# Splitting the selected and local branches' query and key banks over 128 rows in a fused attention and FFN layer

## The chip, the cores and the metric

The kernel runs on one core of a Trainium2 chip. The metric is the device time of one execution in microseconds (us), taken as the median of several runs. A core has TensorE (PE, with its weight loads PEld), VectorE (DVE), ScalarE (ACT), GpSimd (POOL) and SyncE (SP), each working through its own instructions in order, and 16 DMA engines that move data for the queues the engines issue to.

## The reference

One decoder layer on x of 512 rows by 1024 columns, in fp32. A normalised input goes through one wide projection; its columns feed four groups of four heads, which share one output projection; a gated FFN with a causal convolution of width 3 follows.

```python
h = _rms_norm(x, attn_pre_norm[l])
(mq, mk, mv, nq, nkc, nvc, nks, nvs, nkw, nvw, ngate,
 dq, dk, dv, sq, sk, sv) = jnp.split(h @ w_in[l], splits, axis=-1)
o_moba = _moba_attention(...)     # block-sparse, 4 heads of 64
o_nsa  = _nsa_attention(...)      # compressed + selected + window keys; one key head for 4 query heads
o_diff = _diff_attention(...)     # differential: softmax minus lambda times softmax, heads of 32
o_swa  = _swa_attention(...)      # local window of 128 with sinks; 2 key heads for 4 query heads
mix = concatenate([o_moba, o_nsa, o_diff, o_swa], -1)
x = x + _rms_norm(mix @ w_out[l], attn_post_norm[l])
h = _rms_norm(x, ffn_pre_norm[l])
x = x + _rms_norm(_conv_ffn(h, ...), ffn_post_norm[l])
```

Below, NSA is the selected branch, SWA the local one.

## The kernel before, in words

**Precision.** Every fp32 operand is kept as a pair: hi, the value rounded to the matmul's format, and lo, the remainder. A product is three matmuls (hi·hi, lo·hi, hi·lo; `mm3`, L405 to L407 when it is a projection). ACT writes hi, DVE (for some weights POOL) writes lo.

**Weights.** SP loads a unit of weights into a `raw` tile (L91; two buffers, so a load waits until both engines that split the one before last are done with it). ACT makes hi (L152), DVE and POOL lo (L157), into one of four `wu` slots. FFN weights come as `pair` tiles of 1 MB (L104); POOL adds blocks of them into a tile of tag "sum" (L177, two buffers), ACT and DVE split them (L191, L194).

**First half.** A generator yields the projection units group by group (fill_moba, fill_nsa, fill_diff, fill_swa, fill_out). Each unit is 24 matmuls into a PSUM bank; when it ends, small closures that empty the bank are queued (`later`) and are run off one at a time between the matmuls that follow. Attention tasks are woven in at fixed rates: scores (L1012 with the hi of the keys, L1013 with the lo; L1069 for differential heads), softmax (mask and maximum on DVE L955, exponential on ACT L956, normalisation on POOL L948), transposes (L980), weighted sums (L991), combination. NSA's compressed keys need 32 small fp32 products (L733, 31 columns wide). A scheduler then fixes each engine's order from its own simulation of the program, so that fewer or shorter steps on one engine move instructions on others too.

**How a bank of queries or keys is emptied.** A bank holds two heads of 64 rows. For queries, `q_stack` (L475) makes one tile per head that holds hi in one half of its 128 rows and lo in the other: two ACT operations of 64x512 (L481) and two DVE operations (L485) that also scale. For keys, `k_stack` (L490) makes hi in 64 rows (ACT, L498), copies them into the other 64 rows by a DMA on ACT's queue (L499), and puts lo in a second tile whose other half POOL sets to zero (L503, DVE L504). MoBA's four banks, NSA's key bank and two query banks, and SWA's two query banks and key bank are emptied in this way. The differential heads (`narrow_stack`, L823) already do it otherwise: one ACT operation over all 128 rows into a tile `parts` (L833), one DVE operation over 128 rows (L839), and SP DMAs that place the pieces of 32 rows (L830). Their `parts` tiles also have tag "sum", two buffers.

**Second half.** The rest of the output projection, two norms and the FFN, whose products L1319 to L1321 run on `pair` weights.

Of the kernel before, what the change touches and what calls it, by code (L numbers as in the profile page):

```python
# [29 lines left out]
def f32(ap):  # L30
    return ap.bitcast(F32)
# [199 lines left out]
def kernel(  # L231
# [258 lines left out]
    def k_stack(ps, dst, kls, put):  # L490
# [14 lines left out]
            put.append(ts_[a])  # L505
        return [lambda: hi(0), lambda: hi(1), lambda: lo(0), lambda: lo(1)]

    def v_steps(ps, v, v3, t, extra=None):

        dst = v[:, t, :].rearrange("p (r x d) -> p r x d", r=2, x=4)  # L510
        src = ps[:, 0:256].rearrange("p (r x d) -> p r x d", r=2, x=2)
        d3 = v3[:, t, :, :]
        s3 = ps[:, 256:384].rearrange("p (n d) -> p n d", n=2)

        def a0():
            act.activation(dst[:, :, 0::3, :], src, AF.Copy)
            act.activation(d3[:, :, 0:64], s3, AF.Copy)

        def a1():
            act.activation(d3[:, :, 128:192], s3, AF.Copy)  # L520
            if extra:
                extra()

        def b0():
            vec.tensor_sub(dst[:, :, 1:3, :], src, f32(dst[:, :, 0::3, :]))

        def b1():
            vec.tensor_sub(d3[:, :, 64:128], s3, f32(d3[:, :, 0:64]))
        return [a0, a1, b0, b1]
# [90 lines left out]
    pool.memset(pair, 0.0)  # L620
    pool.memset(pair[0:64, 0:1], 1.0)
    pool.memset(pair[64:128, 1:2], 1.0)
    dscale = tab.tile([128, 2], F32, name="dscale")
    for h in range(4):
        pool.memset(dscale[64 * (h % 2):64 * (h % 2) + 64, h // 2:h // 2 + 1], qscale(2, h, 32))
    nsink = tab.tile([128, 4], F32, name="nsink")
    keep(vec.tensor_scalar(nsink, sink, -1.0, None, ALU.mult))
    lprod = tab.tile([128, 2, 32], F32, name="lprod")
# [47 lines left out]
    def fill_nsa():  # L676
# [22 lines left out]
        ps = yield from fm_unit()  # L699
        kls = [tt("kl"), tt("kl")]  # L700
        nks = []
        later(*k_stack(ps, (0, 0), kls, nks))
        later(lambda: nk.extend(zip(nks, kls)))
        mm_done()

# [18 lines left out]
                    vec.tensor_copy(g[:, h, :], g[:, 0, :])  # L724
        for n in range(2):
            ps = yield from fm_unit()
            later(*q_stack(ps, (0, 0), [qscale(1, 2 * n + a, 64) for a in range(2)], nq))
            mm_done()
            while len(xxs) <= n:
                pop()  # L730
# [89 lines left out]
        vec.tensor_sub(ct[1], ps, f32(ct[0]))  # L820
        cmp_["v"], cmp_["p"] = vc, ct

    def narrow_stack(ps, scale, places, twice, put):  # L823


        ts_ = [tt("dd") for _ in range(4)]
        parts = [wst.tile([128, S], F32R, tag="sum", name=nm("parts"), bufs=2) for _ in range(2)]

        def place(n, c, row):
            sp.dma_start(f32(ts_[c][row:row + 32]), f32(parts[n][32 * c:32 * c + 32]))  # L830

        def hi():
            act.activation(parts[0], ps, AF.Copy, scale=scale)  # L833
            for c in range(4):
                place(0, c, 0)
                place(0, c, twice)

        def lo():
            vec.scalar_tensor_tensor(parts[1], ps, scale, f32(parts[0]), ALU.mult, ALU.subtract)  # L839
            for c in range(4):  # L840
                place(1, c, places)
                put.append(ts_[c])
        return [hi, lo]

    def fill_diff():
        for p in range(2):
            ps = yield from fm_unit()
            later(*narrow_stack(ps, dscale[:, p:p + 1], 32, 64, dq))
            mm_done()
            ps = yield from fm_unit()  # L850
            later(*narrow_stack(ps, 1.0, 64, 32, dk))
            mm_done()
# [6 lines left out]
    def fill_swa():  # L859
        for p in range(2):  # L860
            ps = yield from fm_unit()
            later(*q_stack(ps, (64 * p, 64 * p), [qscale(3, 2 * p + a, 64) for a in range(2)], sq_))
            mm_done()
        ps = yield from fm_unit()
        late["skl"] = [tt("kl"), tt("kl")]
        later(*k_stack(ps, (0, 64), late["skl"], sk))
        mm_done()
        yield "swa"

# [616 lines left out]
```

## Time and profile before

| what | value |
|---|---|
| median of 3 runs | 813.96 us (813.44 to 815.26) |
| the profiled execution, its own time | 814.86 us |
| its span, first to last instruction | 813.0 us |
| PE / PEld busy | 776.9 us (96%) / 710.5 us (87%) |
| DVE busy | 658.4 us (81%) |
| ACT busy | 439.2 us (54%) |
| POOL busy | 339.2 us (42%) |
| mean granted TensorE clock | 0.987 |
| q1, the DMA queue with most bytes | 75.81 MB, 30.5% of 16 engines' span |

All positions below are us from the start of the profiled span. Busy shares are means over stages of different kinds; a stage's own limit has to be read from that stage. Names in rows are the program's tile names, and L numbers are lines of the kernel before unless said otherwise. "SPq" and "ACTq" are DMA issues on an engine's queue. fp32 products (transposes L980 and the small L733) leave two records in the trace for each matmul of the program.

### The profile page before, as it was taken

What the parts mean: (1) busy time and instruction counts of PE and PEld (TensorE: products, weight loads), DVE (VectorE), ACT (ScalarE), POOL (GpSimd) and SP (SyncE); (2) the same over time, 40 slices, a digit from 0 to 9 for tenths busy, and PEclk for the clock granted to TensorE, in tenths of its full rate; (3) what the DMA queues carried; (4) which work ended last, traced back from release to release, by engine and by line L of the source; (5) the groups of instructions that cost most, each with busy time, mean ns of one, the idle gap of its engine ahead of it and who ended that gap; (6) DMA issues with size and microseconds to landing.
All of it is one profiled execution on the core that took longest, in us unless ns stands there. A gap on an engine that the chain in (4) does not pass through costs nothing.

```text
span 813.0 us, 13542 instructions
## 1 busy us (share of the span) xinstructions
PE 776.9 (96%) x5087; PEld 710.5 (87%) x5087; DVE 658.4 (81%) x1119; ACT 439.2 (54%) x919; POOL 339.2 (42%) x313
## 2 busy tenths in 40 slices
PE   8999999999988688999999999999999999999995
PEld 8998988998867488988998998998997998998984
DVE  5657678678695999995888797897797897989857
ACT  6657566677685535654645354454354454445532
POOL 5245333437255767323533433442361561563102
PEclk9999999999999879999999999999999999999998
DMA  7455123635132113331132324315206116033212
GB/s 214 119 152 140 49 66 84 169 116 182 54 94 96 70 53 105 104 105 52 53 118 90 105 72 136 105 33 175 91 14 208 44 62 207 6 99 105 75 56 104
DMA packets 74457, 80.87 MB, mean 99 GB/s; under 512 B 8294, under 2 KB 58648, under 8 KB 74392
## 3 DMA queue, kind: packets, MB, share of 16 engines
q1 hardware_dynamic: 72568, 75.81, 30.5%
q10 hardware_dynamic: 1824, 4.20, 1.5%
q8 instruction: 40, 0.66, 0.3%
q14 instruction: 25, 0.20, 0.1%
HBM read 73.71 MB, written 2.10 MB: 93 GB/s over the span
## 4 chain that ended last, share of the span: by engine, by line
PE 63%; DVE 28%; DMA 3%; issue 3%; ACT 2%; POOL 0%; ACTq 0%; DVEq 0%; POOLq 0%; SPq 0%
DVE wu L194 11%; PE mm L405 5%; PE mm L406 5%; PE mm L407 5%; PE tr L406 3%; PE mm L1319 3%; PE mm L1321 3%; PE mm L1320 3%; PE tr L407 3%; DVE y L1369 3%; PE tr L405 3%; PE sc L1319 3%; PE sc L1321 3%; PE sc L1320 3%; PE tr L980 2%
## 5 line engine op out<-in xcount | busy, mean ns | idle before, releaser
L194 DVE TENSOR_TENSOR wu<-pair,wu 128x512 fp32r<-128x512 f32 x188 | 176.2, 972 | 17.4 <-ACT wu L191 17.0
L191 ACT ACTIVATE wu<-pair 128x512 fp32r<-128x512 f32 x188 | 108.5, 622 | 79.2 <-PE sc L1321 21.5
L1321 PE MATMUL mm<-fT,wu 128*128 128x256 f32 x488 | 138.3, 283 | 1.1 <-DVE wu L194 1.1
L1319 PE MATMUL mm<-fT,wu 128*128 128x256 f32 x488 | 138.2, 283 | 0.7 <-ACT mo L1350 0.7
L1320 PE MATMUL mm<-fT,wu 128*128 128x256 f32 x488 | 138.3, 283 | 0.0
L1321 PE MATMUL sc<-fT,wu 128*128 128x256 f32 x392 | 111.2, 284 | 0.0
L1320 PE MATMUL sc<-fT,wu 128*128 128x256 f32 x392 | 111.1, 283 | 0.0
L1319 PE MATMUL sc<-fT,wu 128*128 128x256 f32 x392 | 111.0, 284 | 0.0
L152 ACT ACTIVATE wu<-raw 128x512 fp32r<-128x512 f32 (+2 forms) x126 | 71.2, 610 | 69.5 <-DMA raw<-in_ffn_w_down_dram 36.2
L177 POOL TENSOR_TENSOR sum<-pair 128x512 f32<-128x512 f32 x32 | 47.8, 1497 | 141.8 <-DMA pair<-in_ffn_w_up_dram 65.8
L177 POOL TENSOR_TENSOR pair<-pair 128x512 f32<-128x512 f32 x64 | 104.2, 1640 | 2.0
L177 POOL TENSOR_TENSOR pair<-sum,pair 128x512 f32<-128x512 f32 x32 | 55.8, 1759 | 116.9 <-DVE wu L194 115.0
L157 DVE TENSOR_TENSOR wu<-raw,wu 128x512 fp32r<-128x512 f32 (+2 forms) x96 | 71.7, 764 | 33.0 <-ACT wu L152 32.3
L1321 PEld LDWEIGHTS mm<-fT,wu 128*128 128x128 f32 x488 | 93.6, 192 | 1.6 <-DVE wu L194 1.5
L1319 PEld LDWEIGHTS mm<-fT,wu 128*128 128x128 f32 x488 | 93.6, 192 | 1.2 <-ACT mo L1350 0.9
L1320 PEld LDWEIGHTS mm<-fT,wu 128*128 128x128 f32 x488 | 93.6, 192 | 0.3
L948 POOL TENSOR_SCALAR P<-P,rc 128x128 f32<-128x128 f32 (+2 forms) x80 | 43.2, 559 | 83.4 <-DVE rc L1046 44.6
L1319 PEld LDWEIGHTS sc<-fT,wu 128*128 128x128 f32 x392 | 75.4, 193 | 0.4
L1320 PEld LDWEIGHTS sc<-fT,wu 128*128 128x128 f32 x392 | 75.3, 192 | 0.4
L1321 PEld LDWEIGHTS sc<-fT,wu 128*128 128x128 f32 x392 | 75.3, 192 | 0.0
L956 ACT ACTIVATE P<-P,mn 128x128 f32<-128x128 f32 (+2 forms) x96 | 52.1, 545 | 28.3 <-DVE mn L955 27.9
L157 POOL TENSOR_TENSOR wu<-raw,wu 128x512 fp32r<-128x512 f32 (+2 forms) x30 | 41.7, 1394 | 48.6 <-ACT wu L152 33.9
(321 smaller groups left out, 1944.4 us busy)
## 6 DMA issues: line engine op xcount, KB each, us to landing
pair<-in_ffn_w_gate_dram SPq DMA_DIRECT2D x16, 1024.0 KB, 8.0
pair<-in_ffn_w_up_dram SPq DMA_DIRECT2D x16, 1024.0 KB, 5.4
raw<-in_ffn_w_down_dram SPq DMA_DIRECT2D x32, 512.0 KB, 3.7
raw<-in_w_in_dram SPq DMA_DIRECT2D x14, 512.0 KB, 3.9
raw<-in_w_out_dram SPq DMA_DIRECT2D x8, 512.0 KB, 4.0
dd<-parts SPq DMA_DIRECT2D x48, 64.0 KB, 2.5
raw<-in_w_in_dram SPq DMA_DIRECT2D x10, 256.0 KB, 2.8
x<-in_x_dram SPq DMA_DIRECT2D x4, 512.0 KB, 4.8
```

Source lines behind the costliest of these rows:

```text
L152: keep(self.nc.scalar.activation(box["h"][:, sl], box["r"][:, sl], AF.Copy))
L157: keep(eng.tensor_tensor(box["l"][:, sl], box["r"][:, sl], f32(box["h"][:, sl]), op=ALU.subtract))
L177: self.nc.gpsimd.tensor_tensor(block(g, out), block(g, a), block(g, b), op=op)
L191: self.nc.scalar.activation(box["h"][g], block(g, src), AF.Copy)
L194: self.nc.vector.tensor_sub(box["l"][g], block(g, src), f32(box["h"][g]))
L405: pe.matmul(o, lh, rh, start=first, stop=False)
L406: pe.matmul(o, lh, rl, start=False, stop=False)
L407: pe.matmul(o, ll, rh, start=False, stop=last)
L956: act.activation(pi, pi, AF.Exp, bias=mn[:, i:i + 1], scale=-1.0, accum_out=sm[:, i:i + 1])
L1319: pe.matmul(o, wh, rh, start=first, stop=False, skip_group_check=True)
L1320: pe.matmul(o, wh, rl, start=False, stop=False, skip_group_check=True)
L1321: pe.matmul(o, wl, rh, start=False, stop=last, skip_group_check=True)
```

## The change

NSA's key bank and two query banks and SWA's two query banks and key bank are emptied as the differential heads are: a common helper `both_parts` writes hi of the whole bank in one ACT operation into a `parts` tile and lo in one DVE operation into another, and SP DMAs of 64 rows place the halves. A query bank takes four of these DMAs, a key bank six (hi goes to both halves). The two closures of a query bank replace four. The per-head scales, until now numbers in the code, come from a table `qsc` of six columns, which POOL fills with 12 memsets in place of 4. MoBA's banks stay as they were. The differential heads' keys take lo by a plain subtraction in place of a scaled one.

```diff
+    def both_parts(ps, scale, n, hi_at, lo_at, tiles, done):
+        parts = [wst.tile([128, S], F32R, tag="sum", name=nm("parts"), bufs=2) for _ in range(2)]
+        def place(part, ts_, at):
+            for c, t in enumerate(ts_):
+                for row in at[c]:
+                    sp.dma_start(f32(t[row:row + n]), f32(part[n * c:n * c + n]))
+        def hi():
+            act.activation(parts[0], ps, AF.Copy, scale=scale)
+            place(parts[0], tiles[0], hi_at)
+        def lo():
+            if scale is None or isinstance(scale, float):
+                vec.tensor_sub(parts[1], ps, f32(parts[0]))
+            else:
+                vec.scalar_tensor_tensor(parts[1], ps, scale, f32(parts[0]), ALU.mult, ALU.subtract)
+            place(parts[1], tiles[1], lo_at)
+            done()
+        return [hi, lo]
+    def q_spread(ps, dst, scale, put):
+        ts_ = [tt("qs") for _ in range(2)]
+        return both_parts(ps, scale, 64, [(d,) for d in dst], [(64 - d,) for d in dst], (ts_, ts_),
+                          lambda: put.extend(ts_))
+    def k_spread(ps, dst, kls, put):
+        ts_ = [tt("kk") for _ in range(2)]
+        for d, t in zip(dst, kls):
+            pool.memset(f32(t[64 - d:128 - d]), 0.0)
+        return both_parts(ps, 1.0, 64, [(d, 64 - d) for d in dst], [(d,) for d in dst], (ts_, kls),
+                          lambda: put.extend(ts_))
...
-    dscale = tab.tile([128, 2], F32, name="dscale")
+    qsc = tab.tile([128, 6], F32, name="qsc")
...
-        later(*k_stack(ps, (0, 0), kls, nks))
+        later(*k_spread(ps, (0, 0), kls, nks))
...
-            later(*q_stack(ps, (0, 0), [qscale(1, 2 * n + a, 64) for a in range(2)], nq))
+            later(*q_spread(ps, (0, 0), qsc[:, n:n + 1], nq))
...
-            later(*q_stack(ps, (64 * p, 64 * p), [qscale(3, 2 * p + a, 64) for a in range(2)], sq_))
+            later(*q_spread(ps, (64 * p, 64 * p), qsc[:, 4 + p:5 + p], sq_))
...
-        later(*k_stack(ps, (0, 64), late["skl"], sk))
+        later(*k_spread(ps, (0, 64), late["skl"], sk))
```

The scheduler's orders move with it. Three places follow; in the order after, line numbers are those of the changed kernel (L777 is the small product L733, L1013 the weighted sum L991, L1002 the transpose L980, L1034 the score L1012, L515 a placement, L970 the normalisation L948). Of the tiles, `mm` is a projection's bank, `vb` in L733 that of the small products, `va` a weighted sum, `tr` a transpose, `sc` a score; `parts` are the whole-bank hi and lo, `qs`, `kk`, `kl`, `dd` the operands they are placed in.

**TensorE at the first NSA score.** Before, after the small products of the compressed keys:

```order
L733 MATMUL vb_1069<-xx_973,w_96_920 128x31 x13
L991 MATMUL va_1390<-PT_1156,vm 128x256
L405 MATMUL mm_1111<-hT_0_1_140,wu_866 128x512
L406 MATMUL mm_1111<-hT_0_9_148,wu_866 128x512
L407 MATMUL mm_1111<-hT_0_1_140,wu_866 128x512
L1012 MATMUL sc_1216<-kk_1013,qs_1101 128x128
```

The change, at the same place:

```order
L777 MATMUL vb_1085<-xx_981,w_96_928 128x31 x6
L1013 MATMUL va_1410<-PT_1172,vm 128x256
L777 MATMUL vb_1085<-xx_981,w_96_928 128x31 x2
L1002 MATMUL tr_1423<-ident,P_1041 128x128 x3
L1013 MATMUL va_1410<-PT_1173,vm 128x256
L1013 MATMUL va_1410<-PT_1172,vm 128x128
L1013 MATMUL va_1410<-PT_1173,vm 128x128
L777 MATMUL vb_1085<-xx_981,w_96_928 128x31 x5
L405 MATMUL mm_1126<-hT_0_1_140,wu_874 128x512
```

and, 16 projection matmuls and a transpose row (x3) further, the score:

```order
L407 MATMUL mm_1126<-hT_5_6_145,wu_874 128x512
L1013 MATMUL va_1520<-PT_1382,vm 128x512
L1013 MATMUL va_1520<-PT_1383,vm 128x512
L1034 MATMUL sc_1236<-kk_985,qs_1081 128x128
L1034 MATMUL sc_1349<-kk_985,qs_1081 128x256
```

The score stands behind 18 projection matmuls instead of 3, and the 13 small products are broken up by three transposes and four weighted sums instead of standing in one piece.

**SP's queue around NSA's banks.** Before, only weight loads:

```order
L91 DMA raw_945<-in_w_in_dram 128x8x128
L91 DMA raw_1008<-in_w_in_dram 128x8x128
L91 DMA raw_1089<-in_w_in_dram 128x2x256
L91 DMA raw_1089<-in_w_in_dram 128x2x128
L91 DMA raw_1183<-in_w_in_dram 128x2x256
```

The change:

```order
L91 DMA raw_1025<-in_w_in_dram 128x8x128
L515 DMA kk_986<-parts_989 64x512 x2
L515 DMA kl_983<-parts_990 64x512
L515 DMA kl_984<-parts_990 64x512
L515 DMA qs_1081<-parts_1083 64x512
L515 DMA qs_1082<-parts_1083 64x512
L91 DMA raw_1114<-in_w_in_dram 128x2x256
L91 DMA raw_1114<-in_w_in_dram 128x2x128
L515 DMA qs_1081<-parts_1084 64x512
L515 DMA qs_1082<-parts_1084 64x512
```

The placements stand in one queue with the weight loads; lo of the first query bank (`parts_1084`) stands behind the two loads into `raw_1114`.

**GpSimd around the first pair sums.** Before:

```order
L1007 TENSOR_TENSOR mixl_2323<-mo_2191,mixh_2322 128x512
L177 TENSOR_TENSOR sum_3182<-pair_0_3085 128x512
L177 TENSOR_TENSOR pair_0_3085<-pair_0_3085 128x4x128
L177 TENSOR_TENSOR sum_3184<-pair_1_3087 128x512
L177 TENSOR_TENSOR pair_1_3087<-pair_1_3087 128x4x128
L157 TENSOR_TENSOR wu_2344<-raw_2146,wu_2344 128x512
```

The change:

```order
L546 MEMSET kl_2685 64x512
L546 MEMSET kl_2686 64x512
L157 TENSOR_TENSOR wu_2700<-raw_2429,wu_2700 128x512
L177 TENSOR_TENSOR sum_3214<-pair_0_3117 128x512
L177 TENSOR_TENSOR sum_3216<-pair_1_3119 128x512
L177 TENSOR_TENSOR pair_0_3117<-pair_0_3117 128x4x128
L177 TENSOR_TENSOR pair_1_3119<-pair_1_3119 128x4x128
L970 TENSOR_SCALAR P_2441<-P_2441,rc_2509 128x128
```

The four operations on the first pair move behind SWA's key memsets (L546 here), to just ahead of the normalisation of `P_2441`.

## Rows read from the trace of the kernel before

**Rows 1.** Windows of 20 us: each engine's busy time and instructions, PEclk, DMA share, GB/s.
```profile
180.00:200.00 20.00, 20.00 (x99) 16.71 (x98) 15.76 (x32) 15.38 (x37) 16.81 (x16) 1.00 0.65 212
200.00:220.00 20.00, 20.00 (x101) 16.75 (x99) 14.07 (x44) 13.03 (x33) 5.55 (x6) 1.00 0.25 80
220.00:240.00 20.00, 16.70 (x105) 13.86 (x104) 18.14 (x60) 16.04 (x49) 9.61 (x12) 1.00 0.18 54
```

**Rows 2.** Waits of TensorE, 40 to 222 us (total us, times, longest); the only row.
```profile
PE sc L1012 <- DVE mn L955: 0.9, 1, 0.9
```

**Rows 3.** Single lines: operations that empty banks (ns min/median/max, first and last start).
```profile
L481 ACT ACTIVATE qs<-mm x12: 576/592/596, 28.1 to 192.0; 64x512 fp32r<-64x512 f32 x12
L485 DVE SCALAR_TENSOR_TENSOR qs<-mm,qs x12: 682/690/695, 29.3 to 193.9; 64x512 fp32r<-64x512 f32 x12
L833 ACT ACTIVATE parts<-mm,dscale x2: 670/680/689, 113.3 to 138.9; 128x512 fp32r<-128x512 f32 x2
L839 DVE SCALAR_TENSOR_TENSOR parts<-mm,dscale,parts x2: 732/736/739, 114.7 to 142.3; 128x512 fp32r<-128x512 f32 x2
```

**Rows 4.** Line L499: key copies on ACT's queue (128 KB each); issue, then time to landing.
```profile
L499 ACTq DMA_DIRECT2D kk<-kk x8: 468/481/897, 35.8 to 197.1; - x8
...
DMA to landing us min/median/max: 3.2/4.2/5.2
```

**Rows 5.** Line L830: the differential heads' placements on SP's queue (64 KB each).
```profile
L830 SPq DMA_DIRECT2D dd<-parts x48: 507/585/1268, 115.8 to 158.7; - x48
...
DMA to landing us min/median/max: 2.0/2.5/3.7
```

**Rows 6.** Timeline of SP, 115 to 124.5 us: twelve placements of one bank.
```profile
115.83 7.58 SPq L830 DMA_DIRECT2D dd<-parts  x12
```

**Rows 7.** Timelines of ACT, DVE, POOL and SP around NSA's first query bank, 82 to 88 us.
```profile
84.25 1.19 ACT L481 ACTIVATE qs<-mm 64x512 fp32r<-64x512 f32 x2
...
83.86 1.36 DVE L157 TENSOR_TENSOR wu<-raw,wu 128x512 fp32r<-128x512 f32 x1 [1.22 <-ACT wu L152]
...
84.63 1.72 POOL L157 TENSOR_TENSOR wu<-raw,wu 128x512 fp32r<-128x512 f32 x1
...
82.79 4.47 SPq L91 DMA_DIRECT2D raw<-in_w_in_dram  x3
```

**Rows 8.** Timeline of PE at the first NSA score, 84 to 94 us.
```profile
84.69 2.98 PE L733 MATMUL vb<-xx,w 128*128 128x31 f32 x26
87.51 0.37 PE L991 MATMUL va<-PT,vm 128*128 128x256 f32 x1
...
88.47 0.63 PE L1012 MATMUL sc<-kk,qs 128*128 128x128 f32 x2
...
93.46 0.39 PE L405 MATMUL mm<-hT,wu 128*128 128x512 f32 x1
93.69 0.40 PE L406 MATMUL mm<-hT,wu 128*128 128x512 f32 x1
```

**Rows 9.** Window 88.3 to 91.7 us; columns as in the first group.
```profile
88.30:91.70 3.40, 3.40 (x12) 2.79 (x11) 1.46 (x9) 1.21 (x5) 0.00 (x0) 0.50 0.23 73
```

**Rows 10.** Windows and chain of waits at the second run of small products.
```profile
98.50:102.00 3.50, 3.50 (x34) 3.50 (x33) 3.42 (x7) 1.81 (x4) 2.32 (x3) 1.00 0.02 5
...
100.94 1.71 PE vb L733 x16
```

**Rows 11.** Timelines of POOL, 183 to 232 us, and of DVE, 213 to 218 us.
```profile
184.55 1.29 POOL L177 TENSOR_TENSOR sum<-pair 128x512 f32<-128x512 f32 x1
...
206.16 2.07 POOL L948 TENSOR_SCALAR P<-P,rc 128x128 f32<-128x128 f32 x4 [6.54 <-DVE rc L935]
...
215.61 1.94 DVE L1089 SCALAR_TENSOR_TENSOR P<-P,rc,P 128x128 f32<-128x128 f32 x4
```

**Rows 12.** Timeline of ACT, 195 to 199 us: SWA's key bank; of PE: the first SWA score.
```profile
195.81 1.21 ACT L498 ACTIVATE kk<-mm 64x512 fp32r<-64x512 f32 x2 [1.65 <-PE mm L407]
...
226.32 0.33 PE L1012 MATMUL sc<-kk,qs 128*128 128x128 f32 x1
```

**Rows 13.** Timeline of DVE, 229 to 236 us, behind the differential heads' last scores.
```profile
231.84 3.03 DVE L1089 SCALAR_TENSOR_TENSOR P<-P,rc,P 128x128 f32<-128x128 f32 x4
234.79 0.67 DVE L1002 TENSOR_TENSOR mo<-vb,tmp 64x512 f32<-64x512 f32 x1
```

**Rows 14.** Timeline of POOL, 2 to 8 us: the tables at the start.
```profile
2.52 0.49 POOL L625 MEMSET dscale<- 64x1 f32 x4
...
5.90 0.55 POOL L430 TENSOR_TENSOR rs<-ss,mhalf 128x1 f32<-128x1 f32 x1 [1.57 <-issue]
```

More of the change, by code (lines that the diff above doesn't have):

```diff
@@ L506, in k_stack, with narrow_stack @@
         return [lambda: hi(0), lambda: hi(1), lambda: lo(0), lambda: lo(1)]
+    def both_parts(ps, scale, n, hi_at, lo_at, tiles, done):
[15 more added lines that the diff above has]
+        return [hi, lo]
+    def narrow_stack(ps, scale, places, twice, put):
+        ts_ = [tt("dd") for _ in range(4)]
+        return both_parts(ps, scale, 32, [(0, twice)] * 4, [(places,)] * 4, (ts_, ts_), lambda: put.extend(ts_))
+    def q_spread(ps, dst, scale, put):
[8 more added lines that the diff above has]
+                          lambda: put.extend(ts_))
     def v_steps(ps, v, v3, t, extra=None):
@@ L622 @@
     pool.memset(pair[64:128, 1:2], 1.0)
-    dscale = tab.tile([128, 2], F32, name="dscale")
-    for h in range(4):
-        pool.memset(dscale[64 * (h % 2):64 * (h % 2) + 64, h // 2:h // 2 + 1], qscale(2, h, 32))
+    qsc = tab.tile([128, 6], F32, name="qsc")
+    for m in (1, 2, 3):
+        for h in range(4):
+            c = 2 * m - 2 + h // 2
+            pool.memset(qsc[64 * (h % 2):64 * (h % 2) + 64, c:c + 1], qscale(m, h, (32 if m == 2 else 64)))
     nsink = tab.tile([128, 4], F32, name="nsink")
@@ L821, in compressed @@
         cmp_["v"], cmp_["p"] = vc, ct
[L823 to L843, printed above, removed]
     def fill_diff():
@@ L847, in fill_diff @@
             ps = yield from fm_unit()
-            later(*narrow_stack(ps, dscale[:, p:p + 1], 32, 64, dq))
+            later(*narrow_stack(ps, qsc[:, 2 + p:3 + p], 32, 64, dq))
             mm_done()
```

## The prediction

> **What bounds the kernel now.** I read the page first (TensorE 96% busy, VectorE 81%, the chain of work that ended last mostly on TensorE), then windows of 20 us, then TensorE's own waits, because the change touches six banks that are emptied between about 78 and 198 us and a mean over the span says nothing of that stretch. In it TensorE is busy 20.00 of every 20 us, VectorE 14 to 16, ScalarE 13 to 15 [rows 1]. The list of TensorE's waits from 40 to 222 us has one row, 0.9 us for a mask operation of an attention task [rows 2]; no matmul waits for a query or key bank. From 220 us on this ends: TensorE falls to 16.70 of 20 and VectorE rises to 18.14 [rows 1]. So the place of the change is a stretch where TensorE alone sets the pace, and its matmuls are the same after the change, only in another order. The time of that stretch can change in three ways only: TensorE waits for an operand, its clock differs, or the work behind 220 us starts in another order.
>
> **The change, part by part.**
>
> *Emptying.* Twelve ScalarE operations at 0.592 us (7.1 us) become six at no more than 0.680 us (4.1 us): 3.0 us less. Twelve VectorE operations at 0.690 us (8.3 us) become six at no more than 0.736 us (4.4 us): 3.9 us less [rows 3]. The key banks' operations are counted at the query banks' durations, an estimate. ScalarE's queue also loses four DMA issues of 0.48 us [rows 4]. All of it lies before 200 us, beside a TensorE that never waits for it [rows 2]: 0 us. The SWA banks' share on VectorE, 6 x 0.690 - 3 x 0.736 = 1.9 us, would count only if VectorE were still behind at 220 us; it has 5.9 us idle between 200 and 220 [rows 1], so 0, with -1.9 us as the lower end.
>
> *SP's queue.* Four query banks take 4 placements each and two key banks 6 each, 28 in all, at 0.585 us an issue 16.4 us of queue time, beside the 48 that are there [rows 5]. They are issued one per 0.63 us (7.58 us for 12) [rows 6]. Weight loads now stand behind them, and some placements behind weight loads that wait for a free `raw` tile. The tight one is lo of NSA's first query bank. The bank's hi starts at 84.25 us [rows 7] and ends at 84.93 (0.680 more); two placements go out by 86.1. The two loads into `raw_1114` wait for the split of the weights that held the tile; before, POOL ends it at 84.63 + 1.72 = 86.35 and SP's three loads end at 82.79 + 4.47 = 87.26 [rows 7]. VectorE's lo, after its 83.86 + 1.36, is done by 86.0. So lo's placements go out from 87.3, at 0.585 us each, and land 2.0 to 5.2 us later, between the fastest small placement [rows 5] and the slowest copy of this size [rows 4]: the first score's own tile at 89.3 to 92.5, at the middle 4.2 us 91.5.
>
> When does TensorE want it? At 84.69 us it stands at the small products [rows 8]. Ahead of the score now stand 13 of these, 26 records in 2.82 us up to 87.51; 18 projection matmuls at 0.23 us (93.46 to 93.69), 4.1 us; six transposes of two records at about the 0.11 us of the small products (2.82 over 26), 1.3 us; and six weighted sums, 1920 columns in all, at 0.23 us for 512, 0.9 us [rows 8]. That is 9.1 us: 93.8 us, or some 95.5 if the clock falls as before. The operand is there 1.3 to 4.5 us earlier. I take 0 us; the upper end is +1.4 us, below.
>
> *The clock.* Right after the 26 records of small products in one piece, TensorE was granted 0.50, the 1.2 GHz level, from 88.3 to 91.7 us [rows 8, 9]: 3.4 us in which full speed would have needed 1.7. The second run of small products has 16 records in one piece and kept 1.00 [rows 10]. The change alters both runs. The first is broken into 12, 4 and 10 records, but what stands between is transposes and short weighted sums, and the first projection matmul comes later than before, not earlier: the stretch poor in large products is about as long. The second becomes 10 and 22 records. I take the first fall as staying and no second: 0 us, ends -1.7 and +1.7 us.
>
> *GpSimd.* The four operations on the first FFN pair ran at 184.55 us. Now they share the "sum" tiles with `parts` and stand behind SWA's key bank. That bank's hi starts at 195.81 [rows 12]; six placements and a weight load among them are out by about 202, landed at 205 to 207 with the times of [rows 4]; the second sum and two more at 1.29 us [rows 11] end at about 211. The normalisation behind them, which ran at 206.16 and takes 2.07 us, then ends at about 213 instead of 208.2. VectorE wants it at 215.61 [rows 11]. So some 5 us of delay meet 7.4 us of slack: 0 us. SWA's own banks have more: placed by 207, first score at 226.32 [rows 12].
>
> *The end of the attention.* In VectorE's order a 0.67 us operation, now behind the differential combination at 231.84 us, comes to stand ahead of it [rows 13], and an equally long one moves a few places forward. VectorE is nearly full there, so the bounds are -0.7 and +0.7 us; the work is the same and I take 0.
>
> *Start.* Eight more memsets of POOL at 0.12 us (0.49 for four) are 1.0 us, in front of a pause of 1.57 us before 5.90 us [rows 14]: hidden, 0 us.
>
> **The sum.** 814.86 us for the profiled execution, plus 0. That execution lies 0.9 us above the median of the runs shown, so against the median the forecast is 814.0 us. About 0.2%, 1.6 us, is what a measurement of this kernel can tell from no change.
>
> **The rivals.**
>
> *No clock fall at all.* Pieces of 12, 4 and 10 records are each shorter than the 16 that kept full speed [rows 10]. Against it: no projection matmul stands between them. Time: 814.0 - 1.7 = 812.3 us, and as low as 810.4 if VectorE's 1.9 us counted too.
>
> *A second clock fall.* The second run now has 22 records in one piece, between the 16 that kept the clock and the 26 that lost it [rows 8, 10]. If it decides like the first, and the first stays, TensorE loses another 1.7 us: 815.7 us, slower by 0.21%. It decides when the granted clock shows a second stretch of 0.50 near 100 us. Against it: that stretch held 34 matmuls in 3.5 us before, these 16 among them, and kept 1.00 [rows 10], and the scores put between the new pieces are wide.
>
> *Shared tiles on GpSimd.* The point from which it decides: the first sums end more than 7.4 us later than the normalisation can bear, because a placement of SWA's keys waits behind a weight load. Each further us then goes to the differential heads' transposes on TensorE. With GpSimd's operations at their slower 1.72 us [rows 7] and one more landing of 5.2 us [rows 4] the normalisation would end 3 to 4 us after 215.61: 817 to 818 us. Against it: the estimated 2.6 us to spare.
>
> *Placements one after another.* If the placements of 128 KB took their turn at the rate of the twelve (786 KB in 7.58 us [rows 6], 1.26 us each), the four of the first query bank, from 84.9 us, would be through by 90, and at the longest landing, 5.2 us [rows 4], ready at 95.2: 1.4 us after TensorE's 93.8. Time: 815.4 us. Against it: landings of 64 KB stayed within 3.7 us with twelve in a row [rows 5, 6], and windows of 20 us reach 212 GB/s, twice that rate [rows 1]. The Trainium skill, page "DMA: Bandwidth & Descriptors", section "Rules for kernel authors", says that two transfers to disjoint partition halves serialize, and advises one transfer over 128 partitions; by it the sum would be this rival's 815.4 us, by the landing rows 814.0.
>
> **How the numbers follow.** No change: 0.42. No fall: 0.30. Second fall: 0.12. Shared tiles: 0.09. Placements in turn: 0.07. The first and the last lie within 0.2% of before (0.49 together); terms of a few tenths carry 0.04 of that below the bound and 0.05 above it. No fall lies just outside the bound, and 0.02 of it comes back. Faster is 0.30 - 0.02 + 0.04 = 0.32, slower 0.12 + 0.09 + 0.05 = 0.26, and 0.42 is left for the same. The range reaches from no fall with VectorE's 1.9 us (810.4) to the low end of shared tiles (817.0).
>
> **What would show it.** Right: no row of TensorE's waits up to 220 us beyond about 1 us; one stretch at 0.50 near 88 to 92 us; ScalarE and VectorE busy time lower by 3 to 4 us each; GpSimd's first pair sums at 204 to 211 us. Wrong: TensorE waiting at the first NSA score for a placement; no stretch at 0.50, or two, before 220 us; VectorE's combination near 215 us waiting for GpSimd; or a difference over 2 us that arises behind 220 us, which would mean that the scheduler's new order there matters more than the rows let me see.

## The result, and the profile after

The change makes the kernel slower: 821.46 us (median; 820.84 to 824.02) against 813.7 us (813.07 to 815.26) before, a ratio of 1.0098 [1.0072, 1.0125]. The forecast of 814.0 us and the range up to 817.0 are both missed. The profiled execution took 820.84 us, 6.0 us more than that of before (814.86).

Its page: first busy time, then the chain of work that ended last.

```profile
PE 779.2 (95%) x5087; PEld 710.3 (87%) x5087; DVE 650.1 (79%) x1113; ACT 434.8 (53%) x913; POOL 339.7 (41%) x321
...
PE 58%; DVE 29%; DMA 4%; issue 4%; ACT 3%; POOL 2%; SPq 0%; ACTq 0%; DVEq 0%; POOLq 0%
```

ScalarE and VectorE do less (439.2 and 658.4 us before), as meant. TensorE does the same work (779.2 us busy, 776.9 before); the loss is in waits and in the clock. The windows, against [rows 1, 9] (columns as there), say where:

```profile
88.30:91.70 3.40, 3.26 (x16) 2.43 (x16) 3.30 (x9) 1.66 (x4) 0.00 (x0) 1.00 0.73 183
120.00:140.00 20.00, 18.98 (x112) 16.31 (x112) 16.03 (x51) 11.84 (x33) 7.05 (x13) 1.00 0.37 94
180.00:200.00 20.00, 17.57 (x82) 13.57 (x80) 12.07 (x31) 11.74 (x30) 10.38 (x12) 0.99 0.82 225
200.00:220.00 20.00, 19.70 (x83) 16.21 (x84) 12.57 (x35) 11.90 (x30) 9.51 (x11) 0.84 0.39 105
220.00:240.00 20.00, 18.00 (x101) 14.96 (x99) 15.27 (x48) 15.05 (x42) 9.25 (x9) 1.00 0.34 106
199.60:206.40 6.80, 6.10 (x16) 4.94 (x17) 4.45 (x13) 2.81 (x7) 0.64 (x1) 0.50 0.70 178
```

Where TensorE was busy 20.00 of 20 us, it now stands for 2.4 us (180 to 200) and then runs 6.8 us at half clock: 82 matmuls where there were 99, and 83 where there were 101. The DMA share of 180 to 200 us went from 0.65 to 0.82. The fall of the clock at 88 us is absent in this execution. TensorE's waits, 30 to 225 us, against the single row of [rows 2]:

```profile
PE mm L405 <- DVE parts L525: 2.0, 1, 2.0
PE sc L1034 <- DVE mn L977: 1.8, 2, 1.0
PE vb L1013 <- ACT PT L1005: 0.8, 1, 0.8
```

The first is new: a projection matmul waits for VectorE's emptying of a query bank. Of the two mask waits (`mn`) one was there before; the second falls at 134 us. The first can be followed backwards. First the chain of waits from 186 to 222 us (start, us); then, each alone, the timelines of PE, DVE and ACT (idle time before the row and what ended it in brackets) and of SP:

```profile
190.39 8.99 DMA qs<-parts
199.50 0.76 DVE parts L525
200.30 0.80 PE mm L405
```
```profile
200.30 0.80 PE L405 MATMUL mm<-wu,mixh 128*128 128x512 f32 x1 [1.97 <-DVE parts L525]
```
```profile
199.50 0.75 DVE L525 SCALAR_TENSOR_TENSOR parts<-mm,qsc,parts 128x512 fp32r<-128x512 f32 x1 [3.15 <-DMA qs<-parts]
```
```profile
194.17 1.15 ACT L152 ACTIVATE wu<-raw 128x512 fp32r<-128x512 f32 x2 [2.62 <-DMA raw<-in_w_out_dram]
196.11 0.69 ACT L518 ACTIVATE parts<-mm,qsc 128x512 fp32r<-128x512 f32 x1 [0.78 <-DMA qs<-parts]
```
```profile
181.60 0.42 SPq L104 DMA_DIRECT2D pair<-in_ffn_w_gate_dram  x1
182.11 0.53 SPq L104 DMA_DIRECT2D pair<-in_ffn_w_up_dram  x1
185.44 0.37 SPq L91 DMA_DIRECT2D raw<-in_w_out_dram  x1
187.99 1.14 SPq L515 DMA_DIRECT2D qs<-parts  x2
189.24 0.53 SPq L91 DMA_DIRECT2D raw<-in_w_out_dram  x1
189.82 8.10 SPq L515 DMA_DIRECT2D qs<-parts  x4
```

SP issues the first FFN pair's two loads of 1 MB at 181.6 and 182.1 us and output weights at 185.4 and 189.2. SWA's first query bank is placed in the middle of this. The last placement of its lo, issued at 190.39, lands at 199.38: 9.0 us. Only then is that `parts` tile free, so VectorE, idle for 3.15 us, can write the lo of the *second* query bank, and only then is that bank's PSUM free for TensorE. TensorE's 0.8 us wait for a transposed tile (`PT`), just before, comes from the same stretch: ScalarE had stood 2.62 us for a weight load issued at 185.44 and 0.78 us for a placement of the first bank's hi, and copied that tile late. The placements' own line (L515) says who waited for placements (us, times) and how long they took to land; the same is given below it for the `qs` tiles alone:

```profile
  POOL sum L177: 10.5, 1
  DVE parts L525: 6.6, 2
  ACT parts L518: 3.4, 2
  DVE parts L523: 2.0, 1
...
DMA to landing us min/median/max: 1.9/2.4/9.0
```
```profile
DMA to landing us min/median/max: 2.5/3.0/9.0
```

L515 places the differential heads' pieces too (48 of its 76 DMAs, 32 rows each), and the trace tells the landing of 18 of them only. The 64-row placements among these took 2.3 to 4.4 us, apart from the one of 9.0.

To compare executions I use TensorE's **lag**: its matmuls done up to a time, each counted at the mean cost of its shape in the trace of before, and how much earlier before had done as much. Up to 188 us swa_only runs TensorE in the order of before, and its lag there, 0.2 us at most, says how well the reading holds. Behind 220 us, where TensorE waits more often, the lag jumps by a microsecond or more from one wait to the next. One execution each:

| lag, us | at 130 | 140 | 190 | 210 | 220 | 240 | 260 | 800 |
|---|---|---|---|---|---|---|---|---|
| after | -1.2 | 0.4 | 1.1 | 7.1 | 7.1 | 5.6 | 6.4 | 6.0 |
| nsa_only | 0.2 | 1.5 | 2.5 | 3.7 | 3.7 | 3.8 | 3.5 | 2.6 |
| swa_only | 0.2 | 0.2 | 0.1 | 2.1 | 2.4 | 2.8 | 2.7 | 2.1 |
| late_gate | -1.2 | 0.4 | 1.3 | 2.4 | 2.4 | 4.1 | 4.6 | 3.9 |
| all_part2 | -0.9 | 0.6 | 1.3 | 2.1 | 2.2 | 2.8 | 1.9 | 1.0 |
| nsa_q1 | -1.7 | -1.3 | -1.7 | 2.6 | 2.4 | 2.8 | 2.5 | 1.9 |
| nsa_k | -1.5 | -1.5 | -1.5 | -1.7 | -1.4 | -1.2 | 1.4 | 3.0 |
| swa_late | -1.5 | -1.5 | -1.7 | -1.5 | -1.7 | 2.0 | 1.2 | -0.1 |
| before_late | -1.5 | -1.5 | -1.5 | -1.7 | -1.7 | -1.4 | -2.0 | -2.0 |

The changed kernel loses 1.6 us between 130 and 140 us, 0.7 more up to 190, and 6.0 us between 190 and 210 us; after that nothing. The -1.2 at 130 is in the main the clock fall of [rows 9], which this execution did not have; before_late, which did not have it either, stands at -1.5.

### The profile page after: what moved, and what is told of

Its sections match the earlier page's. It is cut to its first block, busy times and chain, and to the rows that moved or that the text cites. A ratio compares the mean times of both kernels' runs of the same rounds, so it can differ in the third digit from the quotient of the medians.

```text
span 819.1 us, 13585 instructions
## 1 busy us (share of the span) xinstructions
PE 779.2 (95%) x5087; PEld 710.3 (87%) x5087; DVE 650.1 (79%) x1113; ACT 434.8 (53%) x913; POOL 339.7 (41%) x321
## 4 chain that ended last, share of the span: by engine, by line
PE 58%; DVE 29%; DMA 4%; issue 4%; ACT 3%; POOL 2%; SPq 0%; ACTq 0%; DVEq 0%; POOLq 0%
DVE wu L194 11%; PE mm L405 4%; PE mm L406 4%; PE mm L407 4%; PE tr L406 3%; PE mm L1341 3%; PE mm L1343 3%; PE mm L1342 3%; PE tr L407 3%; PE sc L1343 3%; PE sc L1342 3%; PE sc L1341 3%; PE tr L405 3%; DVE y L1391 3%; PE tr L1002 2%
## 5 line engine op out<-in xcount | busy, mean ns | idle before, releaser
L177 POOL TENSOR_TENSOR sum<-pair 128x512 f32<-128x512 f32 x32 | 47.4, 1486 | 149.6 <-DMA pair<-in_ffn_w_up_dram 58.6
L177 POOL TENSOR_TENSOR pair<-sum,pair 128x512 f32<-128x512 f32 x32 | 55.9, 1761 | 119.2 <-DVE wu L194 117.3
L177 POOL TENSOR_TENSOR pair<-pair 128x512 f32<-128x512 f32 x64 | 104.2, 1640 | 1.9
L157 DVE TENSOR_TENSOR wu<-raw,wu 128x512 fp32r<-128x512 f32 (+2 forms) x96 | 68.1, 726 | 40.1 <-ACT wu L152 39.7
L157 POOL TENSOR_TENSOR wu<-raw,wu 128x512 fp32r<-128x512 f32 (+2 forms) x30 | 39.5, 1324 | 71.3 <-ACT wu L152 70.0
L970 POOL TENSOR_SCALAR P<-P,rc 128x128 f32<-128x128 f32 (+2 forms) x80 | 43.7, 565 | 61.2 <-DVE rc L957 23.8
```

The source lines that it names most:

```text
L157: keep(eng.tensor_tensor(box["l"][:, sl], box["r"][:, sl], f32(box["h"][:, sl]), op=ALU.subtract))
L177: self.nc.gpsimd.tensor_tensor(block(g, out), block(g, a), block(g, b), op=op)
```

## The experiments

Theory A: SWA's placements share the DMA engines with the pair loads, land late, and hold `parts` tiles and PSUM banks. Its rivals are A2 (two `parts` tiles are too few, whatever else is under way), B (the placements stand too long in SP's queue) and C (the new order as such). Theory N: NSA's loss comes from the first score that stands behind 15 more projection products. Later came theory D: GpSimd's pair sums, moved, stretch VectorE's differential combination. In kernels with the delay (the `gate` below) line numbers are 4 to 7 higher: L409 is L405, L519 is L515, L1118 is the combination L1111, L181 the sums L177.

**The two halves: nsa_only, swa_only.** One half keeps the old way.

```diff
-            later(*q_spread(ps, (64 * p, 64 * p), qsc[:, 4 + p:5 + p], sq_))
+            later(*q_stack(ps, (64 * p, 64 * p), [qscale(3, 2 * p + a, 64) for a in range(2)], sq_))
-        later(*k_spread(ps, (0, 64), late["skl"], sk))
+        later(*k_stack(ps, (0, 64), late["skl"], sk))
```

(nsa_only; swa_only does the same to the two NSA lines.)

> NSA's three banks are spread over 128 rows, SWA's three are emptied as before. Theory A (SWA's placements land late beside the first 1 MB pair loads, the two parts tiles stay taken, and TensorE stands still for a bank): no stall near 200 us and no half clock there, 812 to 815 us, -0.3% to +0.1% against before. Theory B (the placements stand too long in SP's queue among weight loads, in both branches): part of the loss stays, 816 to 819. Theory C (the scheduler's new order as such): no fixed place for the loss, 816 to 822.

> SWA's three banks are spread, NSA's three are emptied as before. Theory A: the whole loss is here, 819 to 823 us, with TensorE waiting 2 to 3 us for VectorE's lo of SWA's second query bank near 200 us and about 7 us of half clock behind it, and the clock fall at 88 us back. Theory B: about half the loss, 816 to 819. Theory C: no forecast better than 816 to 822, without the wait at that place.

Measured: nsa_only 816.99 us, 1.0036 [1.0017, 1.0056]; swa_only 817.68, 1.0046 [1.0023, 1.0069]. Each half costs 3 to 4 us, together about the whole. Both times lie outside what A expected (812 to 815 and 819 to 823 us) and where B expected them: A had put the whole loss into the SWA half. TensorE's waits, of nsa_only, then of swa_only:

```profile
PE sc L1034 <- DVE mn L977: 1.8, 2, 1.0
PE vb L1013 <- ACT PT L1005: 0.5, 1, 0.5
```
```profile
PE mm L405 <- DVE parts L523: 1.8, 1, 1.8
PE sc L1034 <- DVE mn L977: 0.9, 1, 0.9
```

The second mask wait belongs to the NSA half, the wait for a `parts` tile to the SWA half; in swa_only it is the key bank's (L523), behind placements of the second query bank that took 5.8 us to land, and no half clock follows it. The 88 us clock fall is there in nsa_only (3.4 us at 0.50), whose order of TensorE is that of the changed kernel up to 189 us: whether it comes differs between executions of the same order.

**More tiles: sum3.** The tag "sum" gets three buffers (here and, not shown, in `sum_tile`).

```diff
-        parts = [wst.tile([128, S], F32R, tag="sum", name=nm("parts"), bufs=2) for _ in range(2)]
+        parts = [wst.tile([128, S], F32R, tag="sum", name=nm("parts"), bufs=3) for _ in range(2)]
```

> The changed kernel with a third buffer for the tag of parts and sums. Theory A: VectorE's lo of SWA's second query bank waits for the first bank's hi placements instead of its lo placements, 3 us earlier or more; TensorE's wait near 200 us shrinks to under 1 us, 813 to 816 us. Theory B: the issue times on SP stay as they are and so does the loss, 820 to 823. Theory C: 818 to 823.

**Another queue: actq.** The 64-row placements go out on ScalarE's queue.

```diff
-                    sp.dma_start(f32(t[row:row + n]), f32(part[n * c:n * c + n]))
+                    (act if n == 64 else sp).dma_start(f32(t[row:row + n]), f32(part[n * c:n * c + n]))
```

> The changed kernel with the placements of 64 rows issued on ScalarE's queue instead of SP's. Theory A, where the 16 DMA engines are what is shared: the lo placements of SWA's first query bank still take 6 to 9 us to land while the pair loads are under way, the wait for the parts tile stays, 817 to 822 us. Theory A, where the packets of one queue go in file: they land in 2 to 4 us, no stall, 812 to 815. Theory B: no weight load is ahead of them any more, 812 to 815.

Measured: sum3 823.84 us, 1.0118 [1.0099, 1.0136]; actq 823.47, 1.0131 [1.0079, 1.0184]. Neither helps. sum3 lies above every range that was expected; actq is 1.5 us above that of shared DMA engines, with the landing that this theory expected (6 to 9 us). TensorE's waits and then the placements' landing (line L515) of sum3, and the same of actq:

```profile
PE mm L405 <- DVE parts L523: 3.6, 1, 3.6
```
```profile
DMA to landing us min/median/max: 1.9/2.0/10.1
```
```profile
PE mm L405 <- DVE parts L523: 3.2, 1, 3.2
...
PE mm L405 <- DVE parts L525: 1.5, 1, 1.5
```
```profile
DMA to landing us min/median/max: 1.9/2.1/8.4
```

A third tile moves the wait one bank on, to the key bank. On the other queue the late landing stays, 8.4 us: what is shared is not SP's queue but what lies behind it, and B (812 to 815 us here) falls. The Trainium skill, page "DMA: Bandwidth & Descriptors", section "Issuing engines are not separate DMA queues", says that transfers run on the same 16 DMA engines whichever engine issues them; this run agrees.

**The pair held back: late_gate, swa_late, before_late.** A DMA of 128 bytes out of SWA's last lo tile into each of the first two pair tiles makes their loads wait for SWA's placements. It is put into the changed kernel, into swa_only, and, as a control, into the kernel before.

```diff
+            if self.gate is not None and self.gated < 2:
+                self.gated += 1
+                self.nc.sync.dma_start(t[64:65, 0, 0:32], self.gate())
             self.nc.sync.dma_start(t, srcs[g])
...
-        W.open_pairs(vpool)
+                if (n, t) == (0, 1):
+                    flush()
+                    W.gate = lambda: f32(late["skl"][1])[64:65, 0:32]
+                    W.open_pairs(vpool)
```

> The changed kernel in which the first pair of 1 MB FFN loads is issued only when SWA's last placement has landed (a copy of 32 numbers from that tile into a corner of each pair tile, which the load then overwrites, makes it wait). Theory A (transfers sharing the 16 DMA engines make the placements late): placements land in 2 to 4 us, VectorE's wait for a parts tile near 200 us falls under 1 us, TensorE's wait there goes, 814 to 818 us, the rest being NSA's part as in nsa_only. Theory A2 (two parts tiles are too few whatever else is under way): the waits stay above 2 us, 819 to 823. Theory C (the order as such): 818 to 824.

> swa_only with the same gate on the first pair loads. Theory A: no wait of TensorE for a parts operation, 812 to 815 us. Theory A2: as swa_only, 816 to 819. Theory C: as swa_only or worse.

> Control: the kernel before with the same gate on the first pair loads. All theories: no effect of its own, 813 to 815 us; if it is slower by over 2 us, the gate costs something that late_gate and swa_late carry too.

Measured: late_gate 818.82 us, 1.0067 [1.0045, 1.0088]; swa_late 817.17, 1.0029 [1.0017, 1.0041]; before_late 813.45, 0.9997 [0.9987, 1.0007]. The delay alone costs nothing: before_late is where it was expected. In late_gate the 6.0 us of 190 to 210 us shrink to 1.1, the half clock near 200 us is gone, and four views of late_gate answer to it: TensorE's waits, the placements' line L519, a window, and VectorE's timeline at the second query bank's lo:

```profile
PE mm L409 <- DVE parts L527: 0.5, 1, 0.5
```
```profile
DMA to landing us min/median/max: 1.9/2.6/5.0
```
```profile
200.00:220.00 20.00, 19.49 (x95) 16.17 (x95) 13.59 (x37) 13.95 (x36) 6.04 (x8) 1.00 0.62 173
```
```profile
196.25 0.75 DVE L529 SCALAR_TENSOR_TENSOR parts<-mm,qsc,parts 128x512 fp32r<-128x512 f32 x1 [3.00 <-DMA qs<-parts]
```

For TensorE, theory A is shown: take the loads away from beside the placements, and its wait shrinks to 0.5 us and the half clock goes; in swa_late nothing is lost up to 220 us, where swa_only lost 2.0. One part of A did not come true. VectorE was to wait under 1 us, and it still stands 3.00 us for the first bank's lo, as A2 had it. The last placement of that lo was issued at 190.83 us and VectorE waits for it until 196.2, so it took some 5.3 us; but VectorE goes on 3.25 us earlier than in the changed kernel, and TensorE does not wait for this bank. The times also stay above A's ranges (814 to 818 and 812 to 815 us), since late_gate then loses 1.7 us from 220 to 240, and swa_late, level with before_late up to 220, 3.7 there. VectorE's timeline of late_gate, and then GpSimd's, show what is new:

```profile
219.53 5.95 DVE L1118 SCALAR_TENSOR_TENSOR P<-P,rc,P 128x128 f32<-128x128 f32 x4
```
```profile
220.61 1.34 POOL L181 TENSOR_TENSOR pair<-pair 128x512 f32<-128x512 f32 x1
221.91 1.47 POOL L181 TENSOR_TENSOR sum<-pair 128x512 f32<-128x512 f32 x1
223.46 1.47 POOL L181 TENSOR_TENSOR pair<-pair 128x512 f32<-128x512 f32 x1
```

The combination that took 1.94 us [rows 11] takes 5.95 us with GpSimd's sums beside it; in swa_late 4.93. The 3.03 us of [rows 13] is the same thing on a small scale (1.3 us of GpSimd work beside it). The Trainium skill, page "SBUF — State Buffer", section "Who interferes with whom", says that a VectorE instruction with two SBUF inputs contends with a GpSimd instruction that reads SBUF; the combination reads two, and the trace agrees.

**Other points of delay: late_q, swa_q, nsa_gate.** The gate reads the second query bank's lo instead of the last key lo (late_q in the changed kernel, swa_q in swa_only), or stands in nsa_only as in late_gate.

```diff
-                    W.gate = lambda: f32(late["skl"][1])[64:65, 0:32]
+                    W.gate = lambda: f32(sq_[3])[0:1, 0:32]
```

> The changed kernel with the first pair loads gated on the lo placement of SWA's second query bank instead of the key bank's, some 5 us earlier than in late_gate. Theory A and D together (D: in late_gate POOL's sums of the pair, moved later, fell on VectorE's differential combination and stretched it from 1.9 to 6.0 us): no wait for parts beyond 1 us and a combination near 215 us back under 4 us, 815 to 818 us, NSA's 2 us still in it. If D is wrong: as late_gate, 818 to 821.

> SWA's banks spread, NSA's as before, pair loads gated on the second query bank's lo. Theory A with D: neither the wait near 200 us nor a combination over 4 us, 812.5 to 815 us, equal to before. Without D: as swa_late, 815 to 818. If the placements themselves cost something even without the pair loads: 815 to 818 with VectorE waiting over 2 us for a placement.

> NSA's banks spread, SWA's as before, pair loads gated as in late_gate. Theory A: nsa_only's loss after 180 us was the same collision (weight load behind the pair loads), so about half of it goes: 814 to 816 us, with TensorE's 1 us waits for a mask near 133 us still there. Theory N alone (all of NSA's loss is those waits): as nsa_only, 816 to 818.

Measured: late_q 819.56 us, 1.0066 [1.0048, 1.0084], combination 5.95; swa_q 815.61, 1.0017 [1.0003, 1.003], combination 3.89; nsa_gate 816.91, 1.004 [1.0021, 1.006], combination 3.75. None is in the range that A, with D in the first two, expected (815 to 818, 812.5 to 815 and 814 to 816 us). In late_q the combination did not come free, so it says nothing on D; in swa_q it came under 4 us and the time did not follow. Both say something more on A: here the first 1 MB load runs beside the key bank's placements, and these take 8.1 us (late_q) and 7.4 us (swa_q) to land. Only GpSimd waits for them, and TensorE loses nothing up to 220 us in swa_q: a late landing costs where it is waited for. The delay gives the NSA half nothing back (nsa_only 816.99, from 190 to 210 us 1.2 us lost there and some 0.8 in nsa_gate), as N alone had expected (816 to 818).

**Only NSA's second query bank: nsa_q1.**

```diff
-            later(*q_spread(ps, (0, 0), qsc[:, n:n + 1], nq))
+            later(*(q_spread(ps, (0, 0), qsc[:, n:n + 1], nq) if n else
+                    q_stack(ps, (0, 0), [qscale(1, 2 * n + a, 64) for a in range(2)], nq)))
```

> Only NSA's second query bank is spread; its key bank and first query bank and all of SWA's banks are as before. The first NSA score then stands at its old place in TensorE's order. Theory N (NSA's loss comes from the first score standing 15 products further back, so that NSA's tasks meet at 120 to 135 us, where TensorE then waits for VectorE's masks): no such wait, 813 to 815 us. Theory A for NSA (its placements land late and hold things up): less of it with one bank, 814 to 816 us, with VectorE waiting for a placement.

Measured: 816.9 us, 1.0041 [1.0025, 1.0058], above both ranges. The first score stands where it stood, the second mask wait is gone as N expected, and next to nothing is lost up to 190 us; 4.3 us go between 190 and 210, with not one SWA placement in the program. TensorE's wait and, from ScalarE's timeline, what is behind it:

```profile
PE mm L405 <- DVE qs L485: 2.2, 1, 2.2
```
```profile
192.66 1.16 ACT L152 ACTIVATE wu<-raw 128x512 fp32r<-128x512 f32 x2 [4.91 <-DMA raw<-in_w_out_dram]
```

The new order issues the pair loads at 180.3 and 180.8 us (177.49 and 178.00 before) with a load of output weights right behind them. That load is issued at 181.57 us and ScalarE can start on it 11.1 us later; ScalarE stands 4.9 us for it with SWA's emptying queued behind. So the collision at 180 to 195 us needs no placement: here a weight load that runs beside the two 1 MB loads and is waited for pays.

**What was still open** were two things: whether D is what the delayed kernels lose, and whether N is what the NSA half loses. Four more kernels: nsa_k (only NSA's key bank new), swa_part2 and all_part2 (swa_only and the changed kernel, gate on a later tile), k_part2 (the change without NSA's query banks, same gate).

```diff
-            later(*q_spread(ps, (0, 0), qsc[:, n:n + 1], nq))
+            later(*q_stack(ps, (0, 0), [qscale(1, 2 * n + a, 64) for a in range(2)], nq))
...
+                if (n, t) == (0, 3):
+                    W.gate = lambda: part[2][0][64:65, 0:32]
```

> Leaves only NSA's key bank in the new form; NSA's two query banks and all of SWA are emptied as before. The program's order then puts the first NSA score behind 25 projection products counted from the first small product (27 before, 42 after the change), and the first pair's loads and GpSimd's four sums stand where they stood before. Theory N (the loss of the NSA half comes from the later first score, after which the NSA tasks bunch and TensorE waits for VectorE's masks near 133 us): no mask wait over 1 us at 130 to 140 us, time 812.8 to 814.4 us. Rival (the six placements of the key bank or the two parts tiles cost the time themselves, wherever the score stands): 815.5 to 817 us as with all three banks.

> SWA's banks alone in the new form, the first pair's two loads held back until the third partial tile of the output projection is written, so that GpSimd's four sums fall behind VectorE's second-to-last differential combination. Theory D (with the loads off the placements, what the earlier delayed versions still lost is that combination, stretched from 1.94 to 4.93 us by the sums beside it): the combination near 215 us takes 1.9 to 2.2 us again, the next one may be stretched instead; where neither is, 812.8 to 814.5 us, where the last one (near 232 us) is, 814.5 to 816. Rival (the stretch costs nothing, the loss comes from another change of order behind 220 us): about 817 us as with the earlier delay, whatever the combinations take.

> The whole change with the same later delay of the first pair. Theories A, N and D together: the 3 us that the whole change shares with the NSA half alone stay, the rest goes: 815.5 to 817 us, no wait of TensorE for a parts tile over 0.6 us. If the combination is not what the delayed version lost, 818.5 to 819.5 as before.

> The change without NSA's query banks (NSA's key bank and all of SWA in the new form), with the first pair delayed as in the two above. If N, A and D name all the costs, nothing of the loss is left: 812.5 to 814.5 us, level with before or up to 0.2% faster. If the costs lie elsewhere, 815.5 to 818 us.

Measured: nsa_k 817.96 us, 1.0045 [1.0027, 1.0063]; swa_part2 815.53, 1.0018 [1.0007, 1.003]; all_part2 816.84, 1.0032 [1.0019, 1.0045]; k_part2 815.89, 1.0027 [1.0011, 1.0043].

*nsa_k* lies above N's range (812.8 to 814.4 us) and above its rival's (815.5 to 817), but does what N said of the mechanism. No mask wait is left at 130 to 140 us, and TensorE is 1.2 us ahead of before as late as 240 us. Then it loses 4.2 us to 800, in two stretches at half clock (windows):

```profile
242.80:249.60 6.80, 6.80 (x29) 6.11 (x29) 3.46 (x14) 2.76 (x11) 5.27 (x9) 0.52 0.03 9
280.30:300.80 20.50, 9.43 (x41) 8.34 (x42) 20.50 (x35) 8.85 (x19) 8.93 (x10) 0.51 0.01 4
```

Before, the first is not there and the second lasts 13.7 us. The runs of nsa_k reach from 815.09 us at a mean granted clock of 0.985 to 820.24 at 0.977. Between the two, at 263 us, TensorE waits 2.1 us for the mixing of a head (`PE mm L405 <- ACT mixh L1028`), a wait that before doesn't have. Why the new order brings the fall and the wait is not settled.

*swa_part2 and all_part2.* The sums did not go behind the combination in either, so neither puts D to the test; what they give is sizes. In swa_part2 the sums run beside it again (5.05 us), and 2.5 us go from 220 to 240. In all_part2 most of the sums are over when it starts at 219.93:

```profile
219.93 2.97 DVE L1118 SCALAR_TENSOR_TENSOR P<-P,rc,P 128x128 f32<-128x128 f32 x4
```

The combination is 3.0 us shorter than in late_gate, the loss from 220 to 240 is 0.6 us instead of 1.7, and the median 2.0 us lower, inside the range that was expected. Over the kernels the relation is loose: where that combination took 5.95, 5.95, 5.05, 4.93 and 3.89 us, the lag grew from 220 to 240 us by 1.7, 3.1, 2.5, 3.7 and 2.8 (late_gate, late_q, swa_part2, swa_late, swa_q); where it took 3.0 to 4.0, by 0.3 to 0.9 (before_late, all_part2, nsa_gate, k_part2); in the changed kernel, nsa_only, swa_only, nsa_q1 and nsa_k, where it took 1.94 to 2.15, by 0.4 at most. A second thing differs: late_q, swa_part2, swa_late and swa_q, but not late_gate, have a stretch of 3.5 us at half clock between 225 and 237 us, which the four kernels with 3.0 to 4.0 us have not. (swa_only, nsa_q1 and nsa_k have one between 232 and 240 us as well, at little cost.) In swa_late:

```profile
229.30:232.80 3.50, 3.50 (x19) 3.50 (x17) 2.78 (x13) 1.76 (x6) 1.46 (x3) 0.51 0.44 152
```

How much of the 2.5 to 3.7 us is that fall, and whether the combination brings it about, no run separates. D is supported, not settled.

*k_part2* leaves 0.27%. Its 815.89 us lie in the range for costs that A, N and D do not name (815.5 to 818), not in that for no loss (812.5 to 814.5). It still has a wait of 1.4 us for the key bank's `parts` tile, on which VectorE's step stood 2.83 us; the trace puts that down to ScalarE's copy of a partial output (`part`, L920) and not to a placement. Its runs fall in two groups, six from 813.63 to 814.98 us at 0.989 to 0.990 and six from 816.79 to 819.31 at 0.981 to 0.986.

No version with a new bank beats the kernel before; before_late is level with it.

## Why the prediction was wrong

**The step that failed** is the last sentence on GpSimd and the shared tiles: "SWA's own banks have more: placed by 207, first score at 226.32". The time was some 4 us short (the last placement was issued at 206.45 us, and GpSimd, which waited for it, went on at 210.73), and for the score that did no harm, since it started at 233.31. But the score is not the first to want a placement done. The `parts` tile is wanted first, by the next bank's lo, for which VectorE stood ready at 196.35 us, 8 us after the first bank's; and the PSUM bank behind it is wanted by the next projection matmul. In the old way no tile had to be read out by a DMA before the next bank could be emptied. The prediction followed this tile sharing to GpSimd (its rival of 817 to 818 us) and not to VectorE and ScalarE, which use the same two tiles. In this stretch 6.0 us were lost: 2.0 us of waiting for VectorE, 0.8 for a transposed tile just before, and the rest, some 3, from 6.8 us at half clock. That the fall of the clock follows from the waiting is argued, not shown: in late_gate both are gone, but in swa_only a wait of 1.8 us had no fall behind it.

**The landing time was mis-sized with it.** 2.0 to 5.2 us came from copies that ran at other times [rows 4, 5]. In the window where SWA's placements fall, the DMA engines already stood at 0.65 [rows 1]; beside two loads of 1 MB the landing was 9.0 us and on the other queue 8.4, and some 5.3 once the loads were held back.

**"Emptying ... 0 us"** was right about work and wrong about time: summed over the lines that empty banks, VectorE does 3.9 us less and ScalarE 3.2, as worked out, but these operations became dependent on a landing. (Of VectorE's other 4.4 us, 3.1 are in the 88 weight splits L157, 756 ns each before and 720 after.) "A TensorE that never waits for it" was true of the old dependence only.

**SP's queue** was right at its tight place, with less to spare than worked out. The first NSA score started at 93.60 us (93.8 forecast) and waited for nothing, though its lo placements went out at 90.17 us instead of 87.3; the rival of placements in turn, 815.4 us, fell. The rule that the Trainium skill, page "DMA: Bandwidth & Descriptors", section "Rules for kernel authors", gives for two partition halves cost nothing there. What the step did not ask is what a later first score does to the tasks behind it. TensorE waits 1.0 us for a mask and loses 1.3 to 1.6 us in all at 130 to 140 us in the changed kernel, nsa_only, nsa_gate, late_gate and all_part2; in nsa_q1 and nsa_k, where the score kept its place, there is no such wait and at most 0.4 us is lost. That the tasks bunch behind the later score is the likely reading, but the five kernels are also those with NSA's first query bank in the new form, and no run parts the two.

**The clock.** No second fall near 100 us: right. The first "as staying": an execution of either order may or may not have it, before_late's had none. The term -1.7 us was of the right size (-1.5 in before_late), but it is no property of the change. The fall that did cost came behind the wait at 200 us, a stretch for which the prediction had no clock term.

**GpSimd's sums** were forecast at 204 to 211 us and ran from 210.73 to 215.76, after 10.5 us of waiting for a placement. In the changed kernel this cost nothing that I can see, since TensorE was 7 us late by then and the combination came at 222.97. **The end of attention**: no loss behind 220 us in the changed kernel, as forecast; in the delayed ones there is one (D). **Start**: no lag at 84 us, as forecast.

What stays open: about 1 us that the kernels with all NSA banks new still lose from 190 to 210 us with the pair held back, the tail of nsa_k, the price of D, and what k_part2 loses. The profiled execution's 6.0 us are accounted for by stretch; that the medians differ by 7.8 us is not followed further.

## What to carry to other kernels

When an engine's direct write to a destination is replaced by a write to a staging tile and DMAs, the new due time is not that of the operand's first use but that of the tile's next writer, and through it of the PSUM bank and the matmul behind. Cost the landing from the stretch in which the transfer will run, next to the large loads issued there, not from the same transfer elsewhere. And moving a shared tile moves other engines' work: see what it will run beside.

## What was not expected of the hardware

A placement of 64 rows landed in 2.3 to 4.4 us in most places, and in 8.4 to 10.1 us beside two loads of 1 MB (the changed kernel, actq, sum3); a load of output weights right behind those could be used 11.1 us after its issue (nsa_q1). VectorE's combination of two tiles goes from 1.94 to 5.95 us beside some 4 us of GpSimd's additions. And executions of one and the same program differ by 3 us and more with the mean granted clock (in nsa_only from 814.9 us at 0.989 to 820.4 at 0.983), so that a change of 0.2% needs many of them.
